# Reading 128 rows instead of 64 in the score products of two attentions

## The chip, the cores and the metric

The kernel runs on one core of one Trainium2 chip, as one launch. What is measured is the device time of a launch in microseconds (us), as the median of several runs. One execution has also been recorded by the hardware profiler; its span, from the first to the last instruction, is what the profile's rows cover.

## The reference, cut to what matters

A sequence of 512 tokens with 1024 features passes through two blocks. The first has a pooling mixer, a feed-forward network, a latent attention with a rotary part, and a second feed-forward network. The second has a differential attention and a layer of 16 routed experts. The change touches the scores of both attentions:

```
# latent attention, 8 heads: the score of a query and a key has 128 plain
# features and 64 rotary ones; the rotary key is shared by all heads
q = concatenate([q_nope, q_rope]); k = concatenate([k_nope, k_rope])
s = einsum('bqhd,bkhd->bhqk', qi, k) * sm_scale          # causal, softmax
# differential attention, 8 heads with two maps c of 64 features each
sc = einsum('bqhcd,bkhcd->bhcqk', q[:, s:e], k[:, :e])   # causal, slopes, softmax
pd = p[:, :, 0] - lam * p[:, :, 1]
```

Queries go in blocks of 128, so a block sees 128, 256, 384 or 512 keys.

## The kernel before, in words

**Numbers in two parts.** Every product of 32-bit numbers is made of products of parts in the format float32r: each operand is split into a part `hi` and a part `lo` with `hi + lo` equal to it, and the kernel sums `hi·hi + hi·lo + lo·hi`. Weights stream in by DMA (class `Stream`, queue SP); ScalarE (ACT in the rows) writes `hi`, VectorE (DVE) or GpSimd (POOL) writes `lo`, some pieces ahead of their use.

**Packing the 64 features.** A product on TensorE (PE) reads up to 128 rows of its operands, one feature to a row. A head of the latent attention has only 64 rotary features, and a map of the differential attention only 64 features. So the query is packed: its `hi` lies on one half of the partitions and its `lo` on the other half (`rope` in `mla_project`; `q_parts` in `da_project`). The key's `hi` is there on both halves. One product over 128 rows then gives `hi·hi + lo·hi`. What is still missing is query `hi` times key `lo`, and for this the kernel before takes a second product over the 64 rows where the query's `hi` lies:

```
mm(s, qr[r, q], krl[r, :n], start=False, stop=False)               # mla_scores, L1072
self.mm(pss[c][:, :n], qs[c][r, q], ks[2][r, :n], ...)             # da_scores, L1501
```

In the latent attention the key's `lo` (`krl`) is there on both halves anyway, since the weights of the rotary key stand twice in the matrix. In the differential attention one tile `kl` (third element of `k_parts`) holds the `lo` of map 0 on the lower half and the `lo` of map 1 on the upper half.

**One block of scores.** In the latent attention it takes six products into one PSUM bank: three for the plain features (`kh,qh`, `kl,qh`, `kh,ql`), two for the rotary ones (`krh,..` over 128 rows, `krl,..` over 64), and one bf16 product that adds the causal mask (`mask_b,ident_b`). In the differential attention it takes four products, two maps with a bank each: `kh,qh` (128 rows), `kl,qh` (64), `kl,ql` (128), `kl,ql` (64). In the rows the tiles of a pair are named by the first letter and `h` or `l`, so that `kh` and `kl` are the first and the second of the pair "k", one for each map, and the third tile is named `kl` too.

**What sets the order.** All engines follow an order written out while the program is built. Tasks (`attention`, the projections `da_project`, the output product `out_proj`) are generators; class `Sched` takes the ready task of the lowest rank, and class `Plan` keeps a rough clock for each engine by a list of prices to tell what is ready. On the chip each engine runs its own list in order and waits by semaphores. The projections of later heads and tiles of the output product fill the places where a softmax is waited for.

**Room.** Nearly all working tiles come from one arena of 57 tiles of 128x512. While the second attention runs, weights of the experts are already loaded into it (up to 24 pieces of 128x512, constant `AHEAD`), or as whole chunks of 128x2048 where split weights had been; the SP queue issues them in a fixed order and waits at each until its room is free.

Of the kernel before, what the change touches and what calls it, by code (L numbers as in the profile page):

```python
# [8 lines left out]
F32 = mybir.dt.float32  # L9
# [16 lines left out]
# of the two attentions: query blocks at work at a time; output tiles begun before the last heads  # L26
# are there; output weights loaded ahead (before and after the projections); begun tiles finished
# per whole one; how many query blocks before the end of pair p - 2 the projections of the pairs
# p = 2 and 3 may begin
# [5 lines left out]
# the stream of the experts' weights: pieces in the arena while attending, routing, in the experts;  # L35
# pieces split ahead; chunks in the room of parts before the rows are gathered; chunks that come
# in pieces
# [4 lines left out]
# which parts of a chunk Pool takes the second halves of (feed-forward and first attention; second)  # L42
# [39 lines left out]
class Stream:  # L82
    """Weights in the order of their use: loaded ahead, split into two float32r parts ahead.
    Some are loaded into the arena, and the room of those that are not can take their parts.
    The experts' (from item `first` on) are split and used 512 columns at a time; they are
    loaded into the arena, up to `ahead` such pieces, or where parts had been."""
# [23 lines left out]
    def load(self):  # L110
        """as many of the coming ones as there is room for"""
# [59 lines left out]
    def open(self, t):  # L171
        """the first load after `hold`, and so all that follow, wait for the gathers before it"""
        if self.gate:
            self.net.nc.gpsimd.memset(t[:, :1], 0.0)
            self.gate = False

    def room(self):
        """the tags that the parts of the next one to split can have, if any are free"""
        tags, spare = [], dict(self.spare)
        for tag in ("hi", "lo"):  # L180
            if not spare[tag] and self.arena[self.split]:
                tag = "raw"
            if not spare[tag]:
                return None
            spare[tag] -= 1
            tags.append(tag)
        return tags
# [56 lines left out]
    def gone(self, i, last):  # L244
        """a part of item i is split"""
# [11 lines left out]
    def pump(self, n=1):  # L257
        """n more parts of the splits, as far as there is room"""
# [19 lines left out]
    def release(self, w=None):  # L278
        """the last use of w (or of the longest held) is issued"""
        i = 0 if w is None else [h is w for h, _ in self.held].index(True)  # L280
        for tag in self.held.pop(i)[1]:
            self.spare[tag] += 1
        if self.split >= self.first:
            self.load()
# [16 lines left out]
    def piece(self):  # L301
        """the next 512 columns of the experts' weights"""
# [7 lines left out]
class Plan:  # L310
    """What is issued, on each engine's line of time by a rough price list: when a tile will
    be there, so that a piece that needs it is issued no earlier."""
# [43 lines left out]
    def dma(self, price, *outs):  # L356
        """a transfer (into `outs`)"""
# [40 lines left out]
class Sched:  # L398
    """Interleaves tasks (generators) in program order. A task yields a tile that its next
    piece needs, or how long to wait; the first ready task of the lowest rank goes next."""  # L400
# [31 lines left out]
class Direct:  # L432
    """The weights of one expert whose number is known at run time only."""
# [20 lines left out]
class Net:  # L454
# [21 lines left out]
    def get(self, tag, n=1):  # L476
        """n PSUM banks, when as many are free"""
# [6 lines left out]
    def put(self, tag, n=1):  # L484
        """the last use of n banks is issued"""
# [18 lines left out]
    def hilo(self, hi, lo, src):  # L504
        """hi + lo = src"""
# [3 lines left out]
    def split(self, hi, lo, src, g=None):  # L509
        """hi + lo = src, or src * g, as a task"""  # L510
# [10 lines left out]
    def hilo_g(self, hi, lo, src, g):  # L521
        """hi + lo = src * g, g one number per partition"""
# [40 lines left out]
    def square_sum(self, key, src, first, scale=1.0, eng=None):  # L563
        """adds src^2 (one feature tile) to the sum of the norm"""
# [9 lines left out]
    def col_sums(self, key, ps=None):  # L574
        """sums of the squares per token, [token of the tile, tile], in PSUM"""
# [17 lines left out]
    def bcast(self, col, name, ps=None):  # L593
        """[token of the tile, tile] -> [every partition, token]"""
# [10 lines left out]
    def new_norm(self, gname, keep=False):  # L605
        """the parts of the coming norm's x; the ones in use stay with who holds the lists"""
# [4 lines left out]
    def prep(self, d, eng=None):  # L611
        """the split of x * gain, and the sum of squares, of feature tile d"""
# [4 lines left out]
    def norm_hooks(self):  # L617
        """what the first products of a phase leave to the tensor engine in between"""
# [8 lines left out]
    def pool_mixer(self):  # L627
        """tasks"""
# [122 lines left out]
    def ffn(self, l, hooks, after, extra=None):  # L751
        """x += down(silu(h gate) * (h up)); calls after(d) when x[d] is done"""
# [58 lines left out]
    def rope_tables(self):  # L811
        """cos, and sin with the sign of the rotation, [rotary feature of two heads, token], in
        steps"""
# [37 lines left out]
    def rotated(self, t):  # L851
        """t, rotated"""
# [25 lines left out]
    def norm_task(self):  # L878
        """the factors of the norm of x, on every partition"""
# [8 lines left out]
    def mla_down(self):  # L888
        """tasks: the products with w_down, and the norms of what they give"""
# [83 lines left out]
    def mla_project(self, p, out):  # L973
        """q, k, v of heads 2p and 2p + 1"""
# [24 lines left out]
        def rope(ps):  # L999
            """of each head hi on its half of the partitions, lo on the other"""  # L1000
# [54 lines left out]
    def mla_scores(self, d, hd, qb, h, done):  # L1055
        """a block of queries: scores, softmax; spawns what follows"""
# [3 lines left out]
        r = slice(hd * 64, (hd + 1) * 64)  # L1060
# [11 lines left out]
        mm(s, qr[r, q], krl[r, :n], start=False, stop=False)  # L1072
# [18 lines left out]
    def p_transposed(self, pts, u):  # L1091
        """the probabilities of two query blocks as [key of the block, (key block, query)]"""
# [42 lines left out]
    def attention(self, project, scores, values, keys, most, ahead=0):  # L1135
        """the heads in order, block of queries by block; the projections of the next pair of
        heads and the first output tiles go where the softmax is waited for"""
# [59 lines left out]
    def out_weights(self, name):  # L1197
        """of heads 0 to 5 for two output tiles at a time, of the last two for all"""
# [3 lines left out]
    def out_proj(self, after, most):  # L1202
        """tasks: x += o w; the part of the first heads is added while the last ones are at work"""
# [88 lines left out]
    def tables(self):  # L1292
        """steps"""
# [31 lines left out]
    def da_norm(self):  # L1325
        """the product of the two norms' factors per token; the first one's on x"""
# [29 lines left out]
    def da_project(self, p, out):  # L1356
# [41 lines left out]
        def q_parts(pt):  # L1398
            """for each of the two maps: hi on its half of the partitions, lo on the other"""
# [13 lines left out]
        def k_parts(pt):  # L1413
            """for each of the two maps: hi on both halves of the partitions; lo of both"""
            res, g = (*self.pair("k"), self.tmp("kl", F32R)), self.vec("kg")
# [4 lines left out]
            for i in range(2):  # L1420
                nc.scalar.activation(res[i][halves[1 - i]], res[i][halves[i]].bitcast(F32),
                                     AF.Copy)
                nc.vector.scalar_tensor_tensor(res[2][halves[i]], pt[halves[i]], g[halves[i]],
# [3 lines left out]
            yield res  # L1427
            return res

        def v_part(jj, ps):  # L1430
            """for each token tile: of each head hi, then lo"""
# [33 lines left out]
        for s in range(3):  # L1465
# [3 lines left out]
            if early:  # L1469
                # the last tile of x comes late: the others' products first  # L1470
# [17 lines left out]
    def da_scores(self, d, hd, qb, h, done):  # L1488
# [9 lines left out]
        for c in range(2):  # L1498
            r = slice(c * 64, c * 64 + 64)
            self.mm(pss[c][:, :n], qs[c][:, q], ks[c][:, :n], start=True, stop=False)  # L1500
            self.mm(pss[c][:, :n], qs[c][r, q], ks[2][r, :n], start=False, stop=True)  # L1501
# [77 lines left out]
    def moe_weights(self):  # L1579
        """the gate of an expert goes before the down product of the one before, and so does the  # L1580
        last one's up"""
# [12 lines left out]
    def moe_tables(self):  # L1594
        """constants of the routing; the rows that take what no token owns"""
# [33 lines left out]
    def route_tile(self, d):  # L1629
        """what a finished tile of the residual gives to the norm, the router, the output and  # L1630
        the rows that the experts take"""
# [72 lines left out]
    def route(self):  # L1704
        """tasks: the experts of each token, and its place among each expert's; the first rows"""
# [18 lines left out]
        # rank of each among its four: how many before it are as large, how many after it larger  # L1724
# [48 lines left out]
    def route_weights(self, ps, lg, rank, og, ogb):  # L1773
        """the weight of each token for its two experts; how many rounds the fullest needs"""
# [62 lines left out]
    def slots(self, parts, set_rows):  # L1837
        """token row, weight and norm factor of each slot, for the experts whose positions and
        columns of weights are given"""
# [62 lines left out]
    def turned(self, src, n, res):  # L1902
        """hi and lo of src transposed, 128 columns of src at a time"""
# [30 lines left out]
    def product(self, e):  # L1934
        """the sum over k of e's rows times two of the weights"""
# [77 lines left out]
    def experts(self):  # L2013
        """tasks: the experts in turn; the gate of the next before the down product"""
# [183 lines left out]
```

## Time and profile before

| | |
|---|---|
| median of 3 runs | 1588.48 us (1587.77 to 1590.91) |
| span of the profiled execution | 1588.0 us |
| TensorE busy | 1525.1 us (96%), 7752 products |
| VectorE / ScalarE / GpSimd busy | 1016.4 / 773.0 / 504.2 us |
| mean granted TensorE clock | 0.981 |
| latent attention, scores | about 449 to 545 us of the span |
| differential attention, scores | about 987 to 1184 us |
| routing, experts | to 1251 us, and from there to the end |

The span of the profiled execution lies 0.5 us below the median of the runs. In a row of a timeline the first number is the start; the duration of a product is modelled and overlaps the next product, so what a product takes in a stream is read as the distance from its start to the next start (its step). Weight loads for TensorE (PEld) are records of their own. A shape as `64*128 64x512` gives the weights' rows and columns and then the moving operand's rows and columns.

### The profile page before, as it was taken

How to read it: one execution, taken by the hardware profiler on the slowest of the kernel's cores; microseconds unless marked ns; L12 is line 12 of the kernel's file. 1: busy time of each engine (PE TensorE's matmuls, PEld its weight loads, DVE VectorE, ACT ScalarE, POOL GpSimd, SP SyncE). 2: the span in 40 equal slices, each digit the busy share in tenths (PEclk: the TensorE clock that was granted, in tenths of full speed). 3: DMA queues.
4: the chain of work that ended last, by engine and by line, in shares of the span. 5: the costliest groups of instructions: out<-in, count | busy, mean ns of one | idle time of the engine just before them, and what ended most of it. 6: DMA issues, size and time to landing. Idle time of an engine off the chain costs nothing. (4 is left out here: it accounts for less than half of the span.)

```text
span 1588.0 us, 21545 instructions
## 1 busy us (share of the span) xinstructions
PE 1525.1 (96%) x7752; PEld 1238.5 (78%) x7752; DVE 1016.4 (64%) x1668; ACT 773.0 (49%) x1569; POOL 504.2 (32%) x382
## 2 busy tenths in 40 slices
PE   7999999999999999999999999999999699999996
PEld 6788888888878788888888889889868566666664
DVE  5564344445477755443444467887884599999996
ACT  5323222323366633232223345566672378787875
POOL 3322122312241113221223123312221465565653
PEclk9999999999999999999999999999989699999998
DMA  6131323223210223213222232111067889999961
GB/s 237 61 106 55 118 106 106 89 74 103 83 44 29 65 107 119 98 58 123 106 107 71 84 124 81 54 54 67 27 205 260 243 305 357 371 350 352 341 209 29
DMA packets 69934, 221.60 MB, mean 140 GB/s; under 512 B 7616, under 2 KB 16960, under 8 KB 56640
## 3 DMA queue, kind: packets, MB, share of 16 engines
q1 hardware_dynamic: 56448, 201.03, 35.4%
q0 software_dynamic: 4064, 14.16, 3.8%
q10 hardware_dynamic: 9312, 5.01, 1.1%
q8 instruction: 62, 1.02, 0.3%
q14 instruction: 48, 0.39, 0.1%
HBM read 208.63 MB, written 11.53 MB: 139 GB/s over the span
## 5 line engine op out<-in xcount | busy, mean ns | idle before, releaser
L341 POOL TENSOR_TENSOR lo<-raw,hi 128x512 fp32r<-128x512 f32 (+1 forms) x157 | 224.4, 1440 | 714.1 <-ACT hi L341 625.8
L341 PE MATMUL acc<-xh,hi 128*128 128x512 f32 x744 | 290.5, 390 | 0.5 <-ACT xh L341 0.5
L341 PE MATMUL acc<-xl,hi 128*128 128x512 f32 x744 | 289.6, 389 | 0.3 <-DVE xl L341 0.3
L341 PE MATMUL acc<-xh,lo 128*128 128x512 f32 x744 | 289.5, 389 | 0.0
L341 DVE TENSOR_TENSOR wl<-raw,wh 128x512 fp32r<-128x512 f32 x288 | 264.8, 970 | 9.1 <-ACT wh L341 8.8
L341 ACT ACTIVATE hi<-raw 128x512 fp32r<-128x512 f32 (+1 forms) x378 | 208.7, 607 | 86.4 <-issue 59.8
L341 DVE TENSOR_TENSOR lo<-raw,hi 128x512 fp32r<-128x512 f32 (+1 forms) x221 | 211.7, 968 | 19.8 <-ACT hi L341 19.0
L341 ACT ACTIVATE wh<-raw 128x512 fp32r<-128x512 f32 x384 | 212.4, 621 | 16.2 <-PE acc L341 10.4
L341 POOL TENSOR_TENSOR wl<-raw,wh 128x512 fp32r<-128x512 f32 x96 | 143.3, 1493 | 123.8 <-ACT wh L341 88.8
L341 PEld LDWEIGHTS acc<-xh,hi 128*128 128x128 f32 x744 | 139.7, 188 | 29.6 <-ACT xh L341 1.0
L341 PEld LDWEIGHTS acc<-xl,hi 128*128 128x128 f32 x744 | 139.7, 188 | 29.3 <-DVE xl L341 0.6
L341 PEld LDWEIGHTS acc<-xh,lo 128*128 128x128 f32 x744 | 139.6, 188 | 29.1
L341 DVE TENSOR_TENSOR u<-acc,R 128x512 f32<-128x512 f32 x44 | 30.4, 691 | 181.1 <-PE acc L341 181.1
L341 PE MATMUL acc<-hh,hi 128*128 128x512 f32 x352 | 136.9, 389 | 0.0
L341 PE MATMUL acc<-hl,hi 128*128 128x512 f32 x352 | 136.9, 389 | 0.0
L341 PE MATMUL acc<-hh,lo 128*128 128x512 f32 x352 | 136.9, 389 | 0.0
L341 ACT ACTIVATE hh<-t 128x512 fp32r<-128x512 f32 x44 | 27.8, 632 | 218.4 <-DVE t L341 218.4
L341 DVE TENSOR_TENSOR x<-acc,x 128x512 f32<-128x512 f32 x59 | 40.5, 689 | 124.2 <-PE acc L341 124.2
L341 PE MATMUL acc<-hi,xh 128*128 128x256 f32 x384 | 112.7, 293 | 0.0
L341 PE MATMUL acc<-lo,xh 128*128 128x256 f32 x384 | 108.6, 283 | 0.0
L341 PE MATMUL acc<-hi,xl 128*128 128x256 f32 x384 | 108.5, 283 | 0.0
L341 PE MATMUL acc<-wh,teh 128*96 128x512 f32 x256 | 106.7, 417 | 0.0
(308 smaller groups left out, 2915.4 us busy)
## 6 DMA issues: line engine op xcount, KB each, us to landing
raw<-moe_w SPq DMA_DIRECT2D x200, 256.0 KB, 6.6
raw<-moe_w SPq DMA_DIRECT2D x46, 1024.0 KB, 8.4
raw<-ffn_gu SPq DMA_DIRECT2D x43, 1024.0 KB, 4.8
raw<-ffn_dn SPq DMA_DIRECT2D x32, 704.0 KB, 4.1
raw<-da_in SPq DMA_DIRECT2D x12, 1024.0 KB, 4.9
raw<-mla_up SPq DMA_DIRECT2D x4, 832.0 KB, 4.4
raw<-mla_o_a SPq DMA_DIRECT2D x12, 256.0 KB, 4.3
raw<-da_o_a SPq DMA_DIRECT2D x12, 256.0 KB, 4.2
```

The source lines that it names most:

```text
L341: r = f(*args, **kw)
```

## The change

Both products over 64 rows become products over all 128 rows. What the other half adds is query `lo` times key `lo`, a term that the sum did not have before.

- `mla_scores`: the rotary product with `krl` takes `qr[:, q]` and `krl[:, :n]` whole. No tile is added.
- `da_scores`: the second product of a map takes `ks[2 + c]` whole, a tile of its own for each map.
- `k_parts`: allots two tiles (pair "kl": `klh` for map 0 and `kll` for map 1) in place of one. Each map's `lo` is written by VectorE on the half where the map lies, as before, and two new ScalarE copies for each head bring it to the other half, as it is done with `hi`.

The diff, cut to its code (all else in it takes comments away):

```diff
@@ mla_scores
-        r = slice(hd * 64, (hd + 1) * 64)
...
-        mm(s, qr[r, q], krl[r, :n], start=False, stop=False)
+        mm(s, qr[:, q], krl[:, :n], start=False, stop=False)
@@ da_project, k_parts
-            res, g = (*self.pair("k"), self.tmp("kl", F32R)), self.vec("kg")
+            res, g = self.pair("k") + self.pair("kl"), self.vec("kg")
...
-                nc.vector.scalar_tensor_tensor(res[2][halves[i]], pt[halves[i]], g[halves[i]],
+                nc.vector.scalar_tensor_tensor(res[2 + i][halves[i]], pt[halves[i]], g[halves[i]],
...
             self.put("t")
             yield res
+            for i in range(2):
+                nc.scalar.activation(res[2 + i][halves[1 - i]],
+                                     res[2 + i][halves[i]].bitcast(F32), AF.Copy)
+            yield res
             return res
@@ da_scores
-            r = slice(c * 64, c * 64 + 64)
             self.mm(pss[c][:, :n], qs[c][:, q], ks[c][:, :n], start=True, stop=False)
-            self.mm(pss[c][:, :n], qs[c][r, q], ks[2][r, :n], start=False, stop=True)
+            self.mm(pss[c][:, :n], qs[c][:, q], ks[2 + c][:, :n], start=False, stop=True)
```

The number of products is the same. Since the plan counts the new copies, it puts the pieces of the second attention in another order from the first heads on, up to the output product; the order of TensorE in the routing and the experts is as before. Three places show it.

On TensorE, the first block of scores of the differential attention, with 128 keys (sizes are the result's, so the rows read do not show; `klh` and `kll` are the new pair):

```order
 L341 MATMUL pst<-ident,qn 128x128 x4
 L341 MATMUL pss<-kh,qh 128x128
-L341 MATMUL pss<-kl,qh 128x128
-L341 MATMUL pss<-kl,ql 128x128 x2
+L341 MATMUL pss<-klh,qh 128x128
+L341 MATMUL pss<-kl,ql 128x128
+L341 MATMUL pss<-kll,ql 128x128
 L341 MATMUL acc<-hi,xh 128x256
 L341 MATMUL acc<-hi,xl 128x256
```

Four products stand in the same places; the second and the fourth take the new tiles.

On ScalarE, near the end of the differential attention, where the last pair's keys are made (`kh`, `kl` from PSUM, then their copies; `p` are the exponentials of a block, `pth` transposed probabilities, `bias` the slopes of the next head):

```order
 L341 ACTIVATE kh<-kh 64x512
 L341 ACTIVATE kl<-kl 64x512
-L341 ACTIVATE pth<-pst 128x512
-L341 ACTIVATE p,l_9770<-p,nm_9769 128x256 x2
-L341 ACTIVATE pth<-pst 128x384
+L341 ACTIVATE pth<-pst 128x384
+L341 ACTIVATE klh<-klh 64x512
+L341 ACTIVATE kll<-kll 64x512
+L341 ACTIVATE p,l_9863<-p,nm_9862 128x512 x2
+L341 ACTIVATE bias<-brel 128x512
 L341 ACTIVATE oh<-o 128x512 x5
```

The two new copies stand ahead of the exponentials of the seventh head's last block, and the last head's slopes follow.

On the SP queue, the loads of the experts' weights (pieces are 128x512, chunks 128x2048); the pattern comes six times:

```order
 L131 DMA raw<-da_o_b 128x512 x4
 L131 DMA raw<-da_o_a 128x512 x6
-L164 DMA raw<-moe_w 128x512 x28
-L150 DMA raw<-moe_w 128x2048 x4
+L164 DMA raw<-moe_w 128x512 x24
+L150 DMA raw<-moe_w 128x2048 x2
+L164 DMA raw<-moe_w 128x512 x4
+L150 DMA raw<-moe_w 128x2048 x2
 L164 DMA raw<-moe_w 128x512 x4
 L150 DMA raw<-moe_w 128x2048 x4
```

Two chunks are issued four pieces earlier, each time.

## Rows read from the trace of the kernel before

**Rows 1.** Windows: length, busy us (instructions) of PE, PEld, DVE, ACT, POOL; clock, DMA.
```profile
449.00:545.00 96.00, 94.38 (x550) 74.93 (x548) 73.35 (x166) 61.70 (x155) 18.42 (x15) 1.00 0.12 39
980.00:1140.00 160.00, 160.00 (x1173) 144.76 (x1172) 132.70 (x356) 104.81 (x268) 39.66 (x30) 1.00 0.15 52
1140.00:1190.00 50.00, 44.82 (x207) 34.42 (x206) 42.60 (x116) 38.84 (x103) 8.53 (x9) 0.83 0.51 171
1251.00:1588.00 337.00, 301.11 (x1456) 209.77 (x1456) 308.42 (x403) 256.47 (x479) 183.35 (x126) 0.96 0.85 290
```

**Rows 2.** Timeline of PE, a latent attention block, 128 keys: start, duration, operation.
```profile
449.74 0.28 PE L341 MATMUL pss<-kl,qh 128*128 128x128 f32 x1
449.85 0.27 PE L341 MATMUL pss<-kh,ql 128*128 128x128 f32 x1
449.97 0.27 PE L341 MATMUL pss<-krh,rh 128*128 128x128 f32 x1
450.17 0.32 PE L341 MATMUL pss<-krl,rh 64*128 64x128 f32 x1
450.43 0.23 PE L341 MATMUL pss<-mask_b,ident_b 128*128 128x128 bf16 x1
```

**Rows 3.** Timeline of PE, a latent attention block, 512 keys.
```profile
543.21 0.39 PE L341 MATMUL pss<-kh,ql 128*128 128x512 f32 x1
543.44 0.39 PE L341 MATMUL pss<-krh,rl 128*128 128x512 f32 x1
543.75 0.49 PE L341 MATMUL pss<-krl,rl 64*128 64x512 f32 x1
544.18 0.23 PE L341 MATMUL pss<-mask_b,ident_b 128*128 128x128 bf16 x1
```

**Rows 4.** Timeline of PE, a differential attention block, 128 keys.
```profile
1038.87 0.31 PE L341 MATMUL pss<-kh,qh 128*128 128x128 f32 x1
1039.11 0.32 PE L341 MATMUL pss<-kl,qh 64*128 64x128 f32 x1
1039.36 0.58 PE L341 MATMUL pss<-kl,ql 128*128 128x128 f32 x2
1039.87 0.39 PE L341 MATMUL acc<-hi,xh 128*128 128x256 f32 x1
1040.09 0.28 PE L341 MATMUL acc<-hi,xl 128*128 128x256 f32 x1
1040.21 0.28 PE L341 MATMUL acc<-lo,xh 128*128 128x256 f32 x1
```

**Rows 5.** Timeline of PE, a differential attention block, 512 keys.
```profile
1050.71 0.39 PE L341 MATMUL pss<-kh,qh 128*128 128x512 f32 x1
1051.04 0.49 PE L341 MATMUL pss<-kl,qh 64*128 64x512 f32 x1
1051.46 0.92 PE L341 MATMUL pss<-kl,ql 128*128 128x512 f32 x2
1052.31 0.39 PE L341 MATMUL acc<-hi,xh 128*128 128x256 f32 x1
1052.53 0.28 PE L341 MATMUL acc<-hi,xl 128*128 128x256 f32 x1
```

**Rows 6.** Weight loads of score products: ns min/median/max, first and last start, forms.
```profile
L341 PEld LDWEIGHTS pss<-kl,qh x64: 182/188/286, 449.7 to 1181.6; 128*128 128x128 f32 x32, 64*128 64x128 f32 x32
L341 PEld LDWEIGHTS pss<-krl,rh x16: 182/183/183, 450.2 to 532.0; 64*128 64x128 f32 x16
```

**Rows 7.** The key's copies on ACT in `k_parts`: ns min/median/max.
```profile
L341 ACT ACTIVATE kh<-kh x8: 628/630/634, 982.8 to 1152.2; 64x512 fp32r<-64x512 f32 x8
```

**Rows 8.** Timeline of PE, end of the differential attention: idle time before, its releaser.
```profile
1150.29 0.69 PE L341 MATMUL pst<-ident,on 128*128 128x128 f32 x2 [1.53 <-DVE on L341]
```

**Rows 9.** Waits of VectorE, 980 to 1140 us: us in total, times, longest.
```profile
DVE p L341 <- PE pss L341: 3.5, 6, 1.5
```

**Rows 10.** Waits of the SP queue, 1251 us to the end: us in total, times, longest.
```profile
SPq L150 <- DVE wl L341: 99.7, 33, 5.0
```

## What the change does to the time, predicted

> **What bounds the kernel now.** I read the windows by stage first, then TensorE's timeline inside single blocks of scores, then who waits for whom, and last the loads of the experts' weights. In the latent attention TensorE is busy 94.4 of 96 us, and in the differential attention from 980 to 1140 all of 160 us, at the full clock; VectorE is busy 73.4 and 132.7 us there, ScalarE 61.7 and 104.8 [rows 1]. So these two stretches last as long as TensorE's list takes, and a shorter list shortens them, until VectorE is the one that is late. From 1140 to 1190 it is different: TensorE is busy 44.8 of 50 us at a mean granted clock of 0.83, waiting for the last heads' softmax and values [rows 1, 8]. From 1251 on the experts run, with VectorE busy 308 of 337 us and the weights' stream behind it [rows 1]; the change puts nothing there but two chunks of each round earlier in the queue.
>
> Next comes the inside of a block. In the latent attention a product over 128 rows that follows another one takes a step of 0.11 to 0.12 us with 128 keys and 0.23 us with 512 [rows 2, 3]. The product just ahead of the 64-row one takes 0.20 and 0.31, and the 64-row product itself 0.26 and 0.43 [rows 2, 3]. So the loss sits on both sides of a change in the number of rows. In the differential attention such a change stands between any two neighbours, and there all four products are slow: 0.24, 0.25 and twice 0.255 us with 128 keys, 0.33, 0.42 and twice 0.425 with 512; the projection's product behind the block pays too, 0.22 against 0.12 [rows 4, 5]. A weight load lasts 0.18 to 0.19 us with 64 as with 128 rows [rows 6], and the excess of 0.2 us on a 64-row product looks like one such load that nothing covers.
>
> One rule of the Trainium skill would say otherwise. A 128-row product with 512 keys steps 0.23 us behind another of 128 rows [rows 3], while its load takes 0.19 [rows 6]: the load is covered. The page "TensorE: Matmul & The Clock Gate", in Part 3 under "The mechanism", says that a weight load overlaps running products only where the row groups differ; by it a stream of 128-row products would pay every load, and the change would give nothing on TensorE. The trace disagrees for the stream, and what it shows is the reverse, that a load is uncovered where the rows change.
>
> **The change part by part.** Term one, the latent attention. With 128 keys a block loses (0.20 + 0.26) − 2 × 0.115 = 0.23 us, with 512 keys (0.31 + 0.43) − 2 × 0.23 = 0.28 us [rows 2, 3]. I take 0.255 for all; there are 32 blocks, one 64-row load each, 16 of them under each of two names [rows 6]. That is 8.2 us. VectorE then works 73.4 of 88 us, 83%, which is its present share in the differential attention, where TensorE does not wait [rows 1]. I take 7.5, with 4 and 8.2 as ends.
>
> Term two, the differential attention's blocks. With 128 keys the way from the first product to the second projection product is 1.22 us, and in a stream of 128 rows it would be 4 × 0.115 + 0.12 = 0.58: 0.64 less [rows 2, 4]. With 512 keys it is 1.82, and would be 4 × 0.23 + 0.12 = 1.04: 0.78 less [rows 3, 5]. The mean is 0.71 us a block. There are 32 blocks with two 64-row loads each, half of these under the name in rows 6. The first six heads, 24 blocks, lie in the stretch where TensorE never idles: 17.0 us. The other 8 blocks lie in the tail.
>
> What is late next in that stretch is VectorE. With 17 us gone it has 132.7 us of work in 143, or 93%. The trace has no attention at such a load; the nearest row with one is that of the experts, VectorE at 92% and TensorE at 89% [rows 1]. TensorE at 89% here would give 143 / 0.89 = 161 us, no gain at all. But there the stream of weights sets the pace too, and here VectorE is held up by TensorE for only 3.5 of its 27 idle us [rows 9], the rest being waits along chains that begin at TensorE as well. So the ends are 0 and 17; I take 12, nearer to the upper one, because at a load of 83% TensorE waits not once in 160 us.
>
> Term three, what is added. Two ScalarE copies a head, 16 in all, of 0.63 us by the copies of `hi` [rows 7]: 10.1 us. Up to 1140 twelve of them go beside TensorE's work, with ScalarE at 105 + 7.6 of 143 us; they cost nothing there, as projections stand ahead of most blocks. In the tail there is no such cover. The copies of the last two heads, 4 × 0.63 = 2.5 us, stand ahead of the exponentials on ScalarE, and the last head's first block waits for them.
>
> Term four, the tail from 1140 to 1190. Its 8 blocks offer 8 × 0.71 = 5.7 us, of which the idle time takes some, and the copies take 2.5. The order of the pieces changes too, so that idle places move. The clock of 0.83 means that for a third of the stretch TensorE runs at 1.2 instead of 2.4 GHz, which costs about 0.17 × 50 = 8.5 us of full-speed work; the fall comes behind the idle place of 1.53 us ahead of 1150.29 [rows 1, 8]. Other idle places can give that back or cost as much again. Ends: 14 gained, 9 lost. I take 1 gained, near the middle.
>
> Nothing else should move. The fourth tile of `k_parts` takes up to 4 more of the arena's 57, which can delay a load of output weights; I price it at nothing, within the tail's ends. Routing and experts have TensorE's order of before, and start earlier by what was saved.
>
> Sum: 7.5 + 12 + 1 = 20.5 us. From the span of 1588.0 us this gives 1567.5; the median of the runs lies 0.5 us higher, so 1568 us.
>
> **The rivals.**
> (a) VectorE takes over. The differential attention keeps only about a third of its 17 us (6), the latent attention 5, and the tail loses 2.5 by the copies: 8.5 saved, 1579.5 us. For it: 93% load on VectorE. Against it: no wait of TensorE for it now until 1140.
> (b) Everything comes through, and the tail keeps the clock: 8.2 + 17 + 5.7 = 31 us, 1557 us; with the clock given back up to 1549. For it: TensorE at 160 of 160. Against it: the same load on VectorE.
> (c) Slower, through the experts' stream. Six times two chunks are issued four pieces earlier; a chunk waits for its room at the head of the queue, and all pieces behind it wait too. Today chunks wait 3.0 us in the mean (99.7 / 33) and at most 5.0 [rows 10]. If each of the six moves stops the stream for 5.0 us, that is 30 us against 20.5: 1598 us. It decides from 20.5 / 6 = 3.4 us a move. For it: VectorE and the stream leave little slack there. Against it: several transfers are under way at a time, so that a wait of the queue is not yet a stop.
> (d) It does not do what it says: the slow steps belong to something else than the rows, such as the change of bank or of tile. The blocks stay as they are and the tail pays 2.5 us of copies: 1591 us. Against it: in the latent attention all six products go to one bank, and only the two steps at the 64 rows are slow [rows 2, 3]. The rule of the Trainium skill named above ("TensorE: Matmul & The Clock Gate", Part 3, "The mechanism") would bring the time out here too.
>
> **How the numbers follow.** The forecast, 1560 to 1575 as its own range, has a chance of 0.55; (a), up to 1584, 0.22; (b) 0.13; (c) 0.05; (d) 0.05. To leave out no more than 2 in 10, the range takes in most of (a) and the near part of (b): 1555 to 1583. About 0.2% (3.2 us) is what a measurement of this kernel can tell from no change. The forecast, (a) and (b) are faster, (c) is slower, (d) is divided between the same and slower; some of (a)'s weak end goes to the same. So 0.89 faster, 0.04 the same, 0.07 slower.
>
> **What would show it.** In the profile after, the four products of a block step 0.11 to 0.12 us with 128 keys and 0.23 with 512, and the projection's product behind them 0.12; a 0.2 left there would refute terms one and two. Waits of TensorE for VectorE (`p`, `nm`, `ptl`, `on`) between 980 and 1120 show how much of term two is lost. A clock under 0.83 in the tail, or idle places in front of the last head's first block with the new copies as releaser, would show term four on its bad side. The stretch from the gate of the experts' loads to the end should keep its 337 us within a few; more than 345 would speak for (c). A time above 1583 means that VectorE, or an effect of the new order, took what TensorE gave.

## The result, and the profile after

The changed kernel takes 1569.91 us in the median of 4 runs (1568.86 to 1571.07), against 1589.70 us (1587.77 to 1594.94): a ratio of 0.9869, 95% interval 0.9837 to 0.9901. Timed once more beside the last experiments it took 1568.77 us, ratio 0.9866 (0.9845 to 0.9886). The forecast was 1568.

Inside the blocks everything stepped as a stream of 128 rows does. TensorE's timeline of the latent attention after, first a block with 128 keys, then the end of one with 512:

```profile
448.32 0.27 PE L341 MATMUL pss<-kh,ql 128*128 128x128 f32 x1
448.44 0.27 PE L341 MATMUL pss<-krh,rh 128*128 128x128 f32 x1
448.55 0.27 PE L341 MATMUL pss<-krl,rh 128*128 128x128 f32 x1
448.66 0.23 PE L341 MATMUL pss<-mask_b,ident_b 128*128 128x128 bf16 x1
...
536.70 0.40 PE L341 MATMUL pss<-krh,rl 128*128 128x512 f32 x1
536.93 0.39 PE L341 MATMUL pss<-krl,rl 128*128 128x512 f32 x1
537.16 0.23 PE L341 MATMUL pss<-mask_b,ident_b 128*128 128x128 bf16 x1
```

The two steps that were 0.20 and 0.26 us [rows 2] are 0.11 now, and 0.31 and 0.43 [rows 3] are 0.23. The same view of the differential attention, 512 keys:

```profile
1070.65 0.48 PE L341 MATMUL pss<-kh,qh 128*128 128x512 f32 x1
1070.96 0.39 PE L341 MATMUL pss<-klh,qh 128*128 128x512 f32 x1
1071.20 0.40 PE L341 MATMUL pss<-kl,ql 128*128 128x512 f32 x1
1071.43 0.39 PE L341 MATMUL pss<-kll,ql 128*128 128x512 f32 x1
1071.66 0.28 PE L341 MATMUL acc<-hi,xh 128*128 128x256 f32 x1
1071.78 0.28 PE L341 MATMUL acc<-hi,xl 128*128 128x256 f32 x1
```

From the first product to the second of the projection it is 1.13 us, against 1.82 [rows 5] (this block's first step, 0.31, is a long one, as in other blocks with transposes just ahead; the block at 1041.80 has steps of 0.23, 0.24 and 0.23). With 128 keys the same way is 0.65 us, against 1.22 [rows 4]; its start, and the two products of the projection:

```profile
1029.35 0.30 PE L341 MATMUL pss<-kh,qh 128*128 128x128 f32 x1
...
1029.83 0.34 PE L341 MATMUL acc<-hi,xh 128*128 128x256 f32 x1
1030.00 0.28 PE L341 MATMUL acc<-hi,xl 128*128 128x256 f32 x1
```

The projection's product steps 0.17 here, and 0.12 behind 512 keys.

Where the time went is seen on the weight loads. Before, in the block of [rows 5] (start, duration, idle time of the loads before it):

```profile
1050.60 0.19 PEld L341 LDWEIGHTS pss<-kh,qh 128*128 128x128 f32 x1
1051.04 0.18 PEld L341 LDWEIGHTS pss<-kl,qh 64*128 64x128 f32 x1 [0.24 <-issue]
1051.46 0.19 PEld L341 LDWEIGHTS pss<-kl,ql 128*128 128x128 f32 x1 [0.24 <-issue]
1051.89 0.18 PEld L341 LDWEIGHTS pss<-kl,ql 64*128 64x128 f32 x1 [0.25 <-issue]
```

And after, in the block above:

```profile
1070.62 0.19 PEld L341 LDWEIGHTS pss<-kh,qh 128*128 128x128 f32 x1
1070.73 0.19 PEld L341 LDWEIGHTS pss<-klh,qh 128*128 128x128 f32 x1
1070.97 0.19 PEld L341 LDWEIGHTS pss<-kl,ql 128*128 128x128 f32 x1
1071.20 0.19 PEld L341 LDWEIGHTS pss<-kll,ql 128*128 128x128 f32 x1
```

Before, each load starts only together with the record of its own product (1051.04, 1051.46); the first of them comes 0.33 us behind the start of the product ahead, at 1050.71 [rows 5], where a stream's step is 0.23. After, a load starts one product early: that of `klh` at 1070.73, while the product at 1070.65 runs. Nothing waits by a semaphore in either case, so the page counts TensorE as busy throughout.

The windows after, cut as in [rows 1] (latent attention, differential attention up to its last projections, its end, experts):

```profile
447.00:539.00 92.00, 88.35 (x557) 75.24 (x556) 74.22 (x168) 62.28 (x157) 18.80 (x15) 1.00 0.13 41
979.00:1121.00 142.00, 137.94 (x1123) 135.34 (x1122) 126.30 (x347) 107.83 (x272) 41.18 (x31) 1.00 0.16 58
1121.00:1167.00 46.00, 38.27 (x203) 33.02 (x202) 39.11 (x105) 36.23 (x96) 6.20 (x6) 0.81 0.43 140
1230.00:1567.00 337.00, 298.76 (x1456) 208.14 (x1456) 310.17 (x403) 255.92 (x479) 186.93 (x127) 0.96 0.84 290
```

TensorE, which never idled in the differential attention before its end, now does for 4.1 of 142 us, and in the latent attention for 3.7 of 92 us (it was 1.6 of 96). Whom it waits for in the 142 us (us in total, times, longest):

```profile
PE pst L341 <- DVE l L341: 1.6, 1, 1.6
PE pst L341 <- ACT o L341: 1.1, 1, 1.1
PE acc L341 <- DVE lo L341: 0.6, 1, 0.6
PE pst L341 <- DVE ql L341: 0.4, 1, 0.4
PE pst L341 <- DVE p L341: 0.3, 1, 0.3
```

So 2.9 us of these waits end with VectorE and 1.1 with ScalarE.

To compare kernels I cut each profile at four events that all have: the first 64-row (later 128-row) rotary product; the first transpose of the differential attention; its last projection product; and the GpSimd instruction that opens the experts' loads (L174, here called the gate). Lengths in us:

| kernel | rotary product to first transpose | to last projection | to gate | gate to end |
|---|---|---|---|---|
| before | 516.0 | 180.3 | 104.4 | 337.1 |
| changed | 510.7 | 168.4 | 102.6 | 336.9 |
| changed, again (e11) | 510.6 | 168.4 | 100.2 | 336.1 |
| latent part alone (e1) | 510.6 | 180.3 | 104.3 | 336.3 |
| one tile, 128 rows (e2; again, e12) | 510.6; 510.7 | 165.4; 165.4 | 101.9; 100.5 | 339.9; 338.4 |
| copies and order, 64 rows (e3) | 510.7 | 183.7 | 102.9 | 335.9 |
| 64 rows, grouped (e4) | 510.7 | 181.9 | 96.6 | 337.6 |
| e2 and splits on GpSimd (e6) | 511.0 | 164.9 | 101.3 | 338.1 |
| before and VectorE load (e7) | 516.0 | 180.7 | 104.8 | 338.8 |
| e2 and VectorE load (e8) | 510.7 | 169.2 | 104.1 | 338.2 |
| changed, copies on GpSimd (e9) | 510.7 | 172.3 | 103.4 | 337.1 |
| e2 and idle copies (e10) | 510.7 | 169.0 | 103.2 | 336.8 |

The first two columns repeat to a few tenths between kernels with the same order, the last two to 1 to 3 us; the start ahead of the first event varies by 4 us between profiles and follows no kernel (450.2 us before, and 448.9 in e7, the same kernel up to there). So of the 20.9 us between the two spans, 5.3 come from the latent attention, 11.9 from the differential attention up to its last projection, 1.8 from its end, 0.2 from the experts, and 1.7 from the start, which is chance.

### The profile page after: what moved, and what is told of

The parts are those of the page before. It is cut to its first block, busy times and chain, and to the rows that moved or that the text cites. A ratio compares the mean times of both kernels' runs of the same rounds, so it can differ in the third digit from the quotient of the medians.

```text
span 1567.1 us, 21562 instructions
## 1 busy us (share of the span) xinstructions
PE 1495.6 (95%) x7752; PEld 1233.7 (79%) x7752; DVE 1017.4 (65%) x1668; ACT 782.9 (50%) x1585; POOL 508.8 (32%) x382
## 5 line engine op out<-in xcount | busy, mean ns | idle before, releaser
L341 DVE TENSOR_TENSOR wl<-raw,wh 128x512 fp32r<-128x512 f32 x288 | 268.1, 982 | 6.1 <-ACT wh L341 5.7
L341 DVE TENSOR_TENSOR lo<-raw,hi 128x512 fp32r<-128x512 f32 (+1 forms) x221 | 215.9, 987 | 19.6 <-ACT hi L341 18.9
L341 POOL TENSOR_TENSOR wl<-raw,wh 128x512 fp32r<-128x512 f32 x96 | 147.1, 1533 | 119.4 <-ACT wh L341 90.8
L341 PE MATMUL acc<-wl,teh 128*96 128x512 f32 x256 | 102.5, 401 | 3.3 <-POOL wl L341 1.7
```

What stands on the lines that cost most here:

```text
L341: r = f(*args, **kw)
```

## The experiments

The edits are cut to the lines that matter. e2, e4, e6, e8, e10 and e12 take the latent attention's edit of e1 too; e3 and e9 start from the changed kernel, e5 and e7 from the kernel before.

**e1: the latent attention alone.** The rotary product reads all rows; the rest is as before.

```diff
-        mm(s, qr[r, q], krl[r, :n], start=False, stop=False)
+        mm(s, qr[:, q], krl[:, :n], start=False, stop=False)
```

> Only the latent attention's rotary product reads 128 rows; the differential attention is as before, and so is every engine's order. Theory (a 64-row product leaves a weight load uncovered on either side of the change in rows; VectorE takes a part of the gain): the changed kernel began its second feed-forward network 5.5 us earlier than before after the differing start is taken off, so 1589.7 - 5.5 = 1584 us, 1582 to 1586, and steps of 0.11 to 0.12 us with 128 keys. Rival (the time came from the new order of pieces in the second attention, not from the rows): 1589 us, and nothing at the latent attention.

Measured: 1583.42 us, ratio 0.9965 (0.9952 to 0.9978). The first column falls by 5.4 us, the rest stays. The rows did it, with every engine's order untouched.

**e3: copies and order without the rows.** The changed kernel, whose differential attention reads 64 rows again.

```diff
-            self.mm(pss[c][:, :n], qs[c][:, q], ks[2 + c][:, :n], start=False, stop=True)
+            r = slice(c * 64, c * 64 + 64)
+            self.mm(pss[c][:, :n], qs[c][r, q], ks[2 + c][r, :n], start=False, stop=True)
```

> The changed kernel with its copies, its four key tiles and its order, but the differential attention's second product of a map reads 64 rows again. Theory (rows): the four slow steps of a block come back, 0.64 to 0.78 us a block, 32 blocks, less the 4 us that TensorE now waits for others: about 1584 us, 1580 to 1590. Rival (order): it stays within 4 us of the changed kernel's 1569.9, under 1574.

Measured: 1584.04 us, ratio 0.9964 (0.9951 to 0.9978). A block at 1080.24 steps 0.41, 0.43, 0.43 and 0.42 us again. From the first transpose to the last projection it takes 183.7 us: 15.3 more than with 128 rows, and 3.4 more than with the old order and no copies (e1). So the new order and its copies are together a loss here. TensorE idles 1.6 us in that stretch, in one wait for `l` of VectorE ahead of 1087.13, and from 1085 to 1095, around that wait, its mean granted clock is 0.83: part of the time at 1.2 instead of 2.4 GHz, which takes another 1.7 us. The two make up the 3.4. No run has the new order without the copies.

**e2 and e12: 128 rows without copies.** The single tile is read whole, on the old order. The half that is added then multiplies a query's lo with the other map's key lo, in place of the right term.

```diff
-            r = slice(c * 64, c * 64 + 64)
-            self.mm(pss[c][:, :n], qs[c][r, q], ks[2][r, :n], start=False, stop=True)
+            self.mm(pss[c][:, :n], qs[c][:, q], ks[2][:, :n], start=False, stop=True)
```

> Both score products read 128 rows, but the differential attention keeps the single tile with the lo of map 0 on the lower and of map 1 on the upper half: no copies on ScalarE, no fourth tile, and every engine's order as before. The half added then holds a query's lo times the other map's key lo, a term of the size of the rounding, in place of the right one. Theory (rows): the steps fall as in the changed kernel, and without copies ahead of the last head's first block the tail saves some 2.5 us more: 1564 to 1570 us, 1567. Rival (order): the old order brings the old time back but for the latent part, 1584 us or more.

> The kernel with one tile and 128 rows again, beside the changed kernel: 1565 to 1570 us, 2 to 4 us below it, if copies and order cost what the two profiles say; no difference if they were chance. From the first transposed query to the gate 267 us.

> The changed kernel itself, beside the others: 1568 to 1572 us. From the first transposed query to the gate of the experts' loads 271 us again, if the 3.8 us against the kernel with one tile are no chance.

Measured: 1568.01 us, ratio 0.9857 (0.9840 to 0.9875), and 1566.19, ratio 0.9843 (0.9824 to 0.9862). Beside the second, the changed kernel took 1568.77. Both profiles have 165.4 us up to the last projection, against 168.4 twice for the changed kernel: 3.0 us that repeat. They lie ahead of the last projection and not in the tail, where I had expected them. To the gate it is 267.3 and 265.9 us, against 271.0 and 268.6. In the times it is 1.9 and 2.6 us with intervals that overlap, so faster than the changed kernel is likely and not shown. It adds a wrong term of the size of the rounding in place of the right one, so it is a kernel for an explanation first.

**e4: 64 rows, grouped.** Both 128-row products first, then both 64-row ones.

```diff
         for c in range(2):
-            r = slice(c * 64, c * 64 + 64)
             self.mm(pss[c][:, :n], qs[c][:, q], ks[c][:, :n], start=True, stop=False)
+        for c in range(2):
+            r = slice(c * 64, c * 64 + 64)
             self.mm(pss[c][:, :n], qs[c][r, q], ks[2][r, :n], start=False, stop=True)
```

> The latent attention reads 128 rows; the differential attention reads 64 rows as before, but takes both 128-row products of a block first and then both 64-row ones, of the lower and of the upper rows. Theory A (every change of the set of rows leaves a load uncovered, also from lower to upper): three places in place of four are left and the first product is quick; with 512 keys 0.23 + 0.33 + 0.43 + 0.43 + 0.22 = 1.64 against 1.82 us, 0.18 a block, 32 blocks: 1584 - 5 = 1579 us. Theory B (products over different rows run side by side, as the Trainium skill, TensorE: Matmul & The Clock Gate, Part 3, says of row groups): the two 64-row products take the time of one, 1.26 us a block with 512 keys, and the time falls to about 1570.

Measured: 1576.72 us, ratio 0.9921 (0.9905 to 0.9937), between the two. TensorE's timeline of a block with 512 keys decides:

```profile
1113.90 0.40 PE L341 MATMUL pss<-kh,qh 128*128 128x512 f32 x1
1114.13 0.40 PE L341 MATMUL pss<-kl,ql 128*128 128x512 f32 x1
1114.46 0.50 PE L341 MATMUL pss<-kl,qh 64*128 64x512 f32 x1
1114.46 0.49 PE L341 MATMUL pss<-kl,ql 64*128 64x512 f32 x1
1114.89 0.39 PE L341 MATMUL acc<-hi,xh 128*128 128x256 f32 x1
1115.11 0.28 PE L341 MATMUL acc<-hi,xl 128*128 128x256 f32 x1
```

The two 64-row products, of the lower and the upper rows, start together and take the time of one: theory B's mechanism. This agrees with the Trainium skill, "TensorE: Matmul & The Clock Gate", Part 3, "The mechanism", as to differing row groups. The two changes of the number of rows still cost: 0.33 in place of 0.23 ahead of the pair, 0.43 for the pair, 0.22 in place of 0.12 behind. The block takes 1.21 us against 1.82 before. But the total missed B's 1570: the last projection comes no earlier (181.9 us), and the 8 us are gained behind it. The plan had put the pieces in yet another order, which has 23 more products ahead of the last projection and five waits of 0.6 to 1.8 us for VectorE between 1075 and 1089. Behind the first two of them, at 1081 us, the granted clock falls to its lower level. From 1060, from 1076 and from 1100 us on (TensorE's busy time, then the clock behind POOL's):

```profile
1060.00:1076.00 16.00, 15.81 (x125) 14.55 (x124) 13.87 (x38) 10.95 (x29) 4.33 (x4) 1.00 0.46 164
1076.00:1100.00 24.00, 18.35 (x97) 14.94 (x98) 17.79 (x54) 17.46 (x50) 2.83 (x4) 0.72 0.00 1
1100.00:1141.00 41.00, 41.00 (x337) 39.70 (x337) 32.86 (x83) 24.33 (x63) 12.81 (x10) 1.00 0.08 27
```

Of these 24 us TensorE idles 5.7, and a clock of 0.72 takes 0.28 x 24 = 6.7 more. These 12.4 us eat what 24 shorter blocks give, by an estimate from the one above up to 24 x 0.61 = 14.6. So the steps are shown, and the sum is not a measure of them.

**e5: the 64-row product twice.** In the kernel before, the latent attention issues it twice over the same rows (the term with the key's lo is added twice). It ran once, 1601.23 us, and is read for its steps only.

```diff
         mm(s, qr[r, q], krl[r, :n], start=False, stop=False)
+        mm(s, qr[r, q], krl[r, :n], start=False, stop=False)
```

> The kernel before, whose latent attention takes its 64-row product twice in a row over the same rows, so the term with the rotary key's lo is added twice. It is for one step: from the first 64-row product to the second. Theory (a load stays uncovered where the number of rows changes): the product ahead of the pair and the last of the pair stay slow, but between the two the step is that of a 128-row stream, 0.12 us with 128 keys and 0.23 with 512. Rival (each 64-row product pays for itself): 0.26 and 0.43 us.

The timeline of the 512-key block; the two are merged in one row:

```profile
460.00 0.40 PE L341 MATMUL pss<-krh,rh 128*128 128x512 f32 x1
460.32 0.73 PE L341 MATMUL pss<-krl,rh 64*128 64x512 f32 x2
460.99 0.23 PE L341 MATMUL pss<-mask_b,ident_b 128*128 128x128 bf16 x1
```

The pair takes 0.67 us where one took 0.43 [rows 3], so the added 64-row product costs 0.24. With 128 keys it is 0.37 against 0.26, so 0.11. That is what a product of a 128-row stream takes: a 64-row product is no slower than others; the change between 64 and 128 is.

The one step that the expectation names lies between its two theories. A later window of that view, and one of the loads, show the second of the pair:

```profile
460.66 0.39 PE L341 MATMUL pss<-krl,rh 64*128 64x512 f32 x1
460.43 0.19 PEld L341 LDWEIGHTS pss<-krl,rh 64*128 64x128 f32 x1
```

From the first 64-row product to the second it is 0.34 us (0.17 with 128 keys), and from the second on 0.33. The second load starts at 460.43, while the first product runs, so it is covered. The excess of 0.2 us on a single 64-row product thus falls in two halves: 0.1 on the product behind one change of the rows and 0.1 on the product ahead of the next.

**e7 and e8: VectorE's room.** One instruction more in each block, on a tile of its own, in the kernel before (e7) and in that with one tile (e8); the profiles have 32 of 0.42 us, 13.3 us in all.

```diff
+        nc.nc.vector.tensor_tensor(self.extra, self.extra, self.extra, op=OP.max)
         for c in range(2):
             nc.vector.tensor_tensor_reduce(pts[c][:, :n], pss[c][:, :n], bias[:, T - n:],
```

> The kernel before with one more instruction on VectorE in each block of scores of the differential attention, on a tile of its own that nothing else reads (128x256, about 0.42 us, 32 of them, 13.4 us). Theory (TensorE bounds, VectorE has room at 83%): up to 1140 us it is hidden, and the tail pays up to 8 x 0.42 = 3.4: 1590 to 1593 us. Rival (VectorE bounds already): 1598 us and more.

> The same extra VectorE work, 32 x 0.42 us, in the kernel with one tile and 128 rows (1568.0 us). Theory (the shorter list of TensorE has used up VectorE's room): with 10 us more VectorE is at 98% of the stretch, and most of it shows, 8 to 13 us: 1576 to 1581. Rival (VectorE still has room): 1568 to 1572 us, no more than the extra work costs in the kernel before.

Measured: 1590.93 us, ratio 1.0010 (0.9994 to 1.0025), and 1571.91 us, ratio 0.9884 (0.9863 to 0.9906). Before, the load was hidden nearly whole, 0.7 us from the first transpose to the gate, less than I expected. With 128 rows it costs 6.1 us there, 3.8 of them ahead of the last projection, and 3.9 in the times: more than in the kernel before, so the room has shrunk, but about half of what my theory said. VectorE is not used up.

**e6: splits moved to GpSimd.** In e2, 12 lo splits of the second attention's weights go to GpSimd. This was to take 8.4 us off VectorE.

```diff
+            if self.phase == 1 and not eng and i < self.first and self.half_part == 0:
+                self.net.nc.nc.gpsimd.tensor_tensor(lo, r, hi.bitcast(F32), op=OP.subtract)
```

> The kernel with one tile and 128 rows (1568.0 us), of whose weights in the second attention one more part in four has its lo made by GpSimd in place of VectorE: 12 splits of 0.7 us, 8.4 us, leave VectorE, with the order on the other engines kept. Theory (VectorE at over 90% is what holds back the rest of the gain): 1564 to 1567 us. Rival (it is the chain of one head's softmax, or GpSimd is too slow): 1568 us or more.

Measured: 1567.39 us, ratio 0.9845 (0.9822 to 0.9867), against 1568.01 and 1566.19 without. Up to the last projection it gives 0.5 us. But VectorE was not relieved. From the first transpose on, in 165 us, it has 381 instructions in place of e12's 389, and is busy for 148.5 us in place of 148.3 (e12's row stands under e10):

```profile
963.30:1128.30 165.00, 164.37 (x1345) 161.97 (x1344) 148.47 (x381) 118.01 (x295) 57.90 (x44) 1.00 0.18 64
```

The instructions that are left take longer where they meet a split on GpSimd. Here is one on VectorE and the split beside it, then the same instruction in e12:

```profile
1011.40 1.14 DVE L346 TENSOR_TENSOR l<-l,lam 128x1 f32<-128x1 f32 x1
1011.22 1.30 POOL L243 TENSOR_TENSOR lo<-raw,hi 128x512 fp32r<-128x512 f32 x1
1008.73 0.16 DVE L341 TENSOR_TENSOR l<-l,lam 128x1 f32<-128x1 f32 x1
```

In that stretch 14 instructions of VectorE take over 0.3 us more than the median of their kind, and each of them runs beside a split on GpSimd; in e12 there are 9, and so do they. So e6 says nothing on a VectorE with less work, and its theory stays untested.

**e10: the copies' time alone.** e2 with 16 ScalarE copies, two a head, into a tile that nothing reads; order and room as in e2.

```diff
             self.put("t")
+            for i in range(2):
+                nc.nc.scalar.activation(self.extra[halves[1 - i]],
+                                        res[2][halves[i]].bitcast(F32), AF.Copy)
             yield res
```

> The kernel with one tile and 128 rows and with the old order, plus 16 ScalarE copies of the changed kernel's size and place, two a head, into a tile that nothing reads. Theory (ScalarE's time for the copies is what the changed kernel pays against the one with one tile, 3.8 us from the first transposed query to the gate of the experts' loads): 2 to 4 us more than that kernel, timed beside it, of them most after the last projections. Rival (the new order, or the wait for the copies, costs it): within 1 us of it.

Measured: 1569.88 us, ratio 0.9872 (0.9852 to 0.9892), against 1566.19 for e2 beside it (e12): 3.7 us, as the theory said, with intervals that overlap a little. But 3.6 us lie ahead of the last projection (169.0 against 165.4) and not behind it, where I had put most. The windows show it, 165 us from the first transpose on; first e12 (busy us of PE, PEld, DVE, ACT, POOL):

```profile
960.50:1125.50 165.00, 163.64 (x1341) 161.67 (x1340) 148.32 (x389) 117.41 (x293) 45.41 (x34) 1.00 0.18 62
```

then e10, and who TensorE waits for there:

```profile
959.00:1124.00 165.00, 161.46 (x1311) 158.03 (x1310) 144.88 (x381) 121.21 (x296) 45.35 (x34) 1.00 0.17 61
```

```profile
PE acc L341 <- DVE lo L341: 1.6, 2, 1.0
PE pss L341 <- DVE nm L341: 1.4, 2, 1.1
PE pst L341 <- DVE p L341: 0.3, 1, 0.3
```

ScalarE is busy 121 of 165 us, 73%, and still its copies cost. TensorE's waits end with VectorE's `lo`, `nm` and `p`. VectorE has no more work than in e12, but waits 11.4 us for ScalarE in that stretch, against 9.6. That the copies delay VectorE by ScalarE, and TensorE by VectorE, fits both numbers; single waits were not followed back.

**e9: the copies on GpSimd.** In the changed kernel GpSimd takes the place of ScalarE for the two copies; the plan then makes a third order.

```diff
-                nc.scalar.activation(res[2 + i][halves[1 - i]],
-                                     res[2 + i][halves[i]].bitcast(F32), AF.Copy)
+                nc.gpsimd.tensor_copy(res[2 + i][halves[1 - i]],
+                                      res[2 + i][halves[i]].bitcast(F32))
```

> The changed kernel, with the two copies of a key's lo made by GpSimd in place of ScalarE; the plan counts them there, so the order is a third one. Theory (ScalarE's copies ahead of the exponentials cost the end of the second attention some 2 to 4 us): 1566 to 1568 us, if GpSimd's copies of about 1.3 us each come in time. Rival (the cost is a longer chain from the keys to the first block, whoever copies): 1569 us or more, with TensorE's waits for the copies on GpSimd in place of ScalarE.

Measured: 1575.31 us, ratio 0.9908 (0.9891 to 0.9924), 6.5 us worse than the changed kernel beside it. GpSimd's copies took 0.6 us each, not 1.3. Up to the last projection it is 3.9 us longer than the changed kernel, with 5.9 us of idle TensorE, all of it ended by VectorE (`lo`, `ptl`, and 1.1 us by its own `kll`). At its end, from 1118 to 1175 us, TensorE waits 5.3 us for `nm` and 5.1 for `on`, both of VectorE too, not for the copies. The rival's number came true and its waits did not; engine and order changed together, so the cause stays open.

## Why the prediction was right, and where not

- **What bounds, and the steps.** Right. 0.11 and 0.23 us in the blocks after, 0.12 behind those with 512 keys and 0.17 behind those with 128, where I had said 0.12 for both. e1, e2 and e3 show that the rows alone give it: 15 us between e3 and the changed kernel, with the same order, and the same 15 between e1 and e2 on the old one (180.3 to 165.4).
- **Term one, the latent attention.** 7.5 forecast, 5.3 measured, in every kernel that has it. The steps were right; the term was mis-sized because TensorE's idle time there rose by 2.0 us (1.6 to 3.7, waits for the softmax on ScalarE and VectorE), and I had allowed 0.7. The rest, under 1 us, I can't place.
- **Term two, up to the last projection.** 12 forecast, 11.9 measured, but the step from 17 to 12 failed in its reason. I gave 5 us to VectorE's load. e2 has the same steps and the same work on VectorE, and keeps 14.9 of 17.0, with VectorE busy 148 of 165 us and TensorE 164, nowhere near the 89% of the experts' row. So of the 17.0 VectorE's load takes 2.1 us at most, 1.3 of them in waits for its `lo`; that it matters at all is seen in e8. The remaining 3.0 us come with the copies and the new order, and are as much as the copies cost by themselves on the old order in e10 (3.6). That it is the copies in the new order too is argued from that size.
- **Term three, the copies.** Wrong: I priced the first twelve at nothing. They cost 3 to 4 us ahead of the last projection, on an engine at 73%. Two errors met, too much for VectorE and nothing for the copies, so that the sum of terms two and three came out right is luck.
- **Term four, the end.** 1 forecast, 1.8 and 4.2 measured in two profiles of one kernel. The clock was 0.81 in the first (0.83 before) and 0.85 over the same 46 us of the second (1121.3 to 1167.3), and TensorE does wait for the last head's copies, as said; one of its rows in the changed kernel:

```profile
1143.98 0.33 PE L341 MATMUL pss<-klh,qh 128*128 128x128 f32 x1 [0.92 <-ACT klh L341]
```

- **Nothing else.** Right: 337.1 and 336.9 us from the gate on. Rival (c) had its mechanism: chunks wait longer in the SP queue than in [rows 10], after:

```profile
SPq L150 <- DVE wl L341: 117.2, 37, 8.1
```

  17.5 us more of such waiting, and the stage is as long as before. A wait of the queue was not a stop of the stream.
- **Rivals (a), (b) and (d).** (a)'s sign is there in part: 2.9 us of TensorE's waits end with VectorE. But (a) lost 11 of the 17 us, and e2, with the same work on VectorE, loses 2.1. (b) is nearly e2's case, but its blocks give 14.9 and not 17. (d) is refuted by the blocks. The rule of the Trainium skill that the prediction names with it ("TensorE: Matmul & The Clock Gate", Part 3, "The mechanism") has a second case in the same section, a load into the background weight buffer, which the prediction left out; the trace fits that case better, with steps of 0.23 us and loads of 0.19 in a stream of 128 rows.

## What to carry to other kernels

Products over half the rows saved nothing here, where they alternate with full ones: each change in the number of rows lays a weight load bare, and the page of the profile counts that as busy time, so compare steps from start to start. Either fill the rows, or put the narrow products side by side on different rows, which shortened a block from 1.82 to 1.21 us (e4). An added instruction on an engine with room to spare is not free when it delays what the bounding engine's next pieces need. And see in the rows whether an experiment did what it was made for: work moved off VectorE in e6 left VectorE as busy as before.

## What the runs showed of the hardware

- A weight load is covered behind 128 rows after 128 (step 0.23 us with 512 columns, load 0.19), and behind 64 after 64 on the same rows (e5: the load starts while the product ahead runs, and the added product costs 0.24). Across 64 and 128 it is not covered (0.31 to 0.33 ahead of the 64-row product, 0.43 for it, full clock). The Trainium skill's "TensorEngine Tiling (Array Packing)", Key Properties, says that changing the tiling mode drains TensorE; the trace agrees, and gives it the price: about 0.1 us on the product ahead of a change and 0.1 on the one behind it, so 0.2 on a narrow product between two changes.
- Two 64-row products on different halves, into different PSUM banks, start within 0.01 us of each other (e4).
- A VectorE instruction that runs beside a GpSimd split can take longer: 1.14 us in place of 0.16 beside a split of 1.30 us (e6).
- In e4 the granted clock fell to its lower level at 1081 us, behind idle places of TensorE of 1.05 and 0.84 us; it was 0.72 over the 24 us from 1076 on and 1.00 again from 1100 on.
